# Forgetting attention: the correction matmul of the scores over all 128 rows instead of 64, in widths of at least 256 keys, with the first branch's outputs kept in DRAM

## The chip, the cores and the metric

The program runs on one core of one Trainium2 chip. The metric is the time of one execution on the device in microseconds (us); for a kernel it is the median of its runs. The engines are named as in the profile: PE (TensorE matmuls) with PEld (its weight loads), DVE (VectorE), ACT (ScalarE), POOL (GpSimd), SP (SyncE, which here only issues transfers).

## What is computed

One post-norm decoder layer over 1024 tokens of width 1024. Three causal token mixers run on one input projection: A, a gated delta rule (4 heads); B, forgetting attention (8 heads of 64); C, gated linear attention (4 heads). Their outputs are projected, merged by gates and projected once more; memory cross-attention and a routed mixture of experts follow. The part that the change touches is B:

```python
logits = (jnp.einsum('bqhd,bkhd->bhqk', q_blk, kf) * (dh ** -0.5)
          + c_blk[..., :, None] - cum_k[:, :, None, :])
logits = jnp.where(key_pos[None, :] <= query_pos[:, None], logits, -jnp.inf)
p = jax.nn.softmax(logits, axis=-1)
return jnp.einsum('bhqk,bkhd->bqhd', p.astype(v.dtype), v)
```

It is swept in blocks of 128 queries; block number qb sees (qb + 1) * 128 keys.

## The kernel before

**Precision by splitting.** float32 products are made from two parts in the type fp32r: hi is the rounded value, lo the rest. A product is hi*hi + hi*lo + lo*hi, three matmuls into one PSUM tile. `Stream.run` (L127 to L156) makes the input projection this way: for each block of 128 weight columns and each half of the tokens, 24 matmuls of 512 columns (L142, L143, L144). It is cut into steps of six matmuls; the mixers call `k.stream.fill(n)` to put n steps between their own instructions, so that PE has work while another engine prepares the next operand.

**Forgetting attention.** Heads go in pairs, p = 0 to 3. A head is only 64 wide, so hi and lo of its queries share one tile of 128 rows: `u.Q[a]` has hi in the head's own 64 rows and lo in the other 64 (`evq`, L735). `u.K[a]` holds the keys' hi part twice, in both halves (`evk`, L742). One matmul over 128 rows (L777) thus gives (q_hi + q_lo) * k_hi. The term q_hi * k_lo comes from a second matmul into the same PSUM tile (L778), over the head's own 64 rows alone; the keys' lo part `u.kl` is one tile for both heads, each in its own half.

`fox_mix` (L766) goes through the query blocks from 7 down to 0 and through both heads in each: `scores` (L777, L778 in groups of up to 512 keys; then on DVE the bias and the row's minimum, L781, on ACT the exponential, L789, on DVE the scaling, L791), `values` (L805, 64 columns wide, for both heads of a block) and `transposed` (L798), with three stream steps at the end of each round. While pair p is worked on, the stream projects q, k and v of pair p + 1, and gates of the merge. The projection's PSUM tiles and those of `values` come from one pool of two (`pmm`).

**Merge.** While pair 3 is worked on, the stream is `Merge` in place of the projection: it splits the outputs of the branches in the order c (GLA), a (delta rule), b (attention) into hi and lo and multiplies them by their projection weights. The branches' outputs are `oT`. Those of c wait in DRAM (`k.spill = "c"`) and are loaded again (L1025); those of a wait in SBUF, in four tiles taken before the delta rule begins (L2101).

**Room.** All large tiles come from one pool of 45 tiles of 4 KB a partition (`slot`). The order of the instructions on each engine is made by a scheduler, which places what the program records; each engine then goes through its list in order, and a transfer that waits on SP holds those behind it.

Of the kernel before, what the change touches and what calls it, by code (L numbers as in the profile page):

```python
# [8 lines left out]
F32 = mybir.dt.float32  # L9
# [10 lines left out]
D = 1024  # L20
T = 1024
# [23 lines left out]
def slot(k, name, shape=(128, T), dt=F32):  # L45
    """A 4 KB tile of the one pool that all large tiles share."""
    return k.b4.tile(list(shape), dt, tag="b4", name=name)


def split(k, hi, src, lo):  # L50
    """hi + lo = src exactly, each of them an fp32r value."""
    k.nc.scalar.activation(hi, src, AF.Copy)  # L52
    k.nc.vector.tensor_tensor(lo, src, hi.bitcast(F32), op=OP.subtract)  # L53
# [15 lines left out]
def load_w(k, src, cols, nb=ND):  # L69
    """128 columns of a [128 * nb, n] matrix, split: (hi, lo) as [128 rows, nb row blocks, 128]."""  # L70
    return split_raw(k, load_raw(k, src, cols, nb), nb)


def proj_T(k, w, evac, m=128):
    """evac(half, psum[m, 512]) = (x @ w)^T for each half of the tokens."""
# [12 lines left out]
class Stream:  # L88
    """Products of blocks of 128 columns of a weight with a transposed operand, one block a job, in steps between
    which other work can be put. parts: of that operand, lists by row blocks of (hi, lo), by default of x."""  # L90
# [12 lines left out]
    def hold(self, unit):  # L103
        """No job after those of this unit is begun."""
        self.limit = self.ends[unit]

    def load(self, i):
        """Weights of the jobs up to the one after job i, and two more where they are in the large pool."""
        while len(self.w) < len(self.jobs) and (
                len(self.w) < i + 2 or (len(self.w) < i + 4 and self.jobs[len(self.w)][6] is load_big)):  # L110
            src, cols, *_, load = self.jobs[len(self.w)]
            self.w.append(load(self.k, src, cols))

    def run(self):
# [5 lines left out]
        def finish():  # L120
            """What follows the last job; with a lag, when the next one is under way."""
# [46 lines left out]
def rsqrt_steps(k, out, ss, n, eps, scale=1.0, name=None):  # L168
    """Instructions for out = (scale * ss + eps) ** -0.5 on [128, n], by Newton steps from the exponent's guess."""
# [17 lines left out]
def setup(k, ins):  # L187
# [3 lines left out]
    # rows of parameters, turned into columns by one transpose  # L191
# [17 lines left out]
    k.tri = misc[:, 3]                                           # [j, i]: 1 where j <= i  # L209
# [4 lines left out]
def param_columns(k):  # L214
# [5 lines left out]
    # 0.5 from silu's tanh form, sqrt(128) from the mean of the squares  # L220
# [4 lines left out]
def alloc_T(k, half, name="th"):  # L225
    """(hi, lo) of half the tokens of a transposed [1024, tokens] operand: pairs of row blocks of [128, 2, 512]."""
# [3 lines left out]
def transpose_row(k, row, xT, t):  # L230
    """Token block t (natural, [128, 1024]) into its half of the transposed operand, split."""
# [12 lines left out]
def load_x(k, x):  # L244
    """x, transposed and split; the stream's first products come between."""
# [23 lines left out]
def small_block(k, ins):  # L269
    """The narrow columns of w_in: beta and decays of GDN, forget gates of fox, low rank of GLA."""  # L270
# [15 lines left out]
    # --- GDN: token columns of b and a  # L286
# [9 lines left out]
    gb = k.const.tile([128, 2, NT, 4], F32, name="gb")          # G (cumulative), beta  # L296
    # beta = 1 / (1 + exp(-b))
# [13 lines left out]
    # log1p(e) = 2 atanh(e / (2 + e)), e <= 1  # L311
# [21 lines left out]
    # row forms through DRAM: row (what, chunk, head)  # L333
# [8 lines left out]
    # --- fox: minus the cumulative log forget gate, in rows 64..71; GLA: log gates (times 16) of the two pairs of heads  # L342
# [27 lines left out]
    # -log f = ln(1 + exp(-|z|)) - min(z, 0)  # L370
# [16 lines left out]
def gdn_setup(k):  # L387
# [6 lines left out]
    k.negm = masks[:, 7]                                         # [j, i]: 0 where j <= i, NEG elsewhere  # L394
    nc.gpsimd.memset(k.negm, 0.0)
    nc.gpsimd.affine_select(k.negm, k.negm, [[1, 128]], OP.is_ge, NEG, base=0, channel_multiplier=-1)
    # what the inverse by blocks of 32 rows takes: L^T's diagonal blocks, four times over, and columns of T^T's
# [3 lines left out]
    # and its operands that are zero outside of the diagonal blocks of 32  # L401
# [9 lines left out]
# words of a chunk's [128, 128] in DRAM, so that its four diagonal blocks and the next chunk's are equally far apart  # L411
# [7 lines left out]
def blocks32(flat, g):  # L419
    """Rows g, g + 4, .. of the diagonal blocks [(chunk, block), 8, 32]."""  # L420
# [44 lines left out]
def gdn_mix(k, u, h, oT):  # L465
# [8 lines left out]
    # row forms of G and beta of the head  # L474
# [35 lines left out]
    def norms(y, scale, name, keep=()):  # L510
        """1 / norm of scale ** 0.5 * y by tokens; keeps y in natural form."""
# [12 lines left out]
    # k: to natural form, normalised, and back  # L524
# [9 lines left out]
    def with_k(xT, out, by, places=((slice(0, 128), slice(0, 4)),)):  # L534
        """out = (k times x)^T, weighted."""
# [9 lines left out]
    # L^T with its column blocks of 32 in the order 0, 2, 3, 1  # L545
    LT = c3(G.LT)
    with_k(kT, LT, BB, ((slice(0, 64), slice(0, 4, 3)), (slice(64, 128), slice(1, 3))))
    # T = (I + L)^-1; Tt is its transpose. The diagonal blocks of 32 rows by substitution, a quarter of the columns of
    # T on each quarter of the partitions
# [12 lines left out]
    # beta * v in natural form  # L562
# [4 lines left out]
    # q is left as it is, and the output divided by its norm  # L567
    rq = norms(yq, 128.0, "g_rq")
    # k with the decay to the chunk's end; q with the decay from its start
# [17 lines left out]
    # and the others by doubling the inverted diagonal blocks: blocks 3 and 1 of 32 rows by 2 and 0, of T in Te, of T^T  # L587
    # in Tp
    b = [slice(32 * i, 32 * i + 32) for i in range(4)]
    Te, Tp, Xp = G.Te, G.Tp, G.Xp  # L590
    Tu, X = c3(G.X[:, 0:HALF]), c3(G.X[:, HALF:])                # T's upper half of 64, and L T of it
# [32 lines left out]
    # the scan over the chunks  # L624
# [31 lines left out]
    finish_out(k, on, u.sz, 74, oT, c3(G.X))  # L656


def finish_out(k, on, sz, wc, oT, sq, spill=None):
    """RMS norm over the 128 features of on [tok, chunk, 128], times silu, transposed into oT."""  # L660
# [20 lines left out]
def fox_tiles(k, i):  # L681
    """Operands of one pair of heads; there are two sets."""
# [3 lines left out]
    F.kl.append(slot(k, "f_kl", dt=F32R))  # L686
# [9 lines left out]
def fox_setup(k):  # L696
# [4 lines left out]
    # minus the cumulative log forget gate of a head, in all rows  # L701
# [7 lines left out]
def fox_bias(k, p, a, b):  # L709
    """Loads it, for head a of pair p, from key block b up to where it has been loaded."""  # L710
# [4 lines left out]
def fox_mask(k, qb, a):  # L715
    """Masks it for query block qb; only blocks before that are read without afterwards."""
# [4 lines left out]
def fox_proj(k, ins, p, u):  # L721
    """Pair p of heads. Head 0 has its hi parts in rows 0..63 of Q and lo in 64..127, head 1 reversed."""
# [19 lines left out]
    def evk(half, ps):  # L742
        s = slice(half * HALF, (half + 1) * HALF)
        for a, own, other in ((0, up, dn), (1, dn, up)):
            nc.scalar.copy(u.K[a][own, s], ps[own])
            nc.vector.tensor_tensor(u.kl[own, s], ps[own], view(u.K[a], F32)[own, s], op=OP.subtract)
# [19 lines left out]
def fox_mix(k, u, p, oT):  # L766
# [3 lines left out]
    def scores(qb, a):  # L770
        own = (up, dn)[a]
# [3 lines left out]
        for g in range((n + 511) // 512):  # L775
            ks = slice(g * 512, min(n, g * 512 + 512))
            nc.tensor.matmul(S[:, ks], u.Q[a][:, qs], u.K[a][:, ks], start=True, stop=False)  # L777
            nc.tensor.matmul(S[:, ks], u.Q[a][own, qs], u.kl[own, ks], start=False, stop=True)  # L778
# [41 lines left out]
def gla_set(k):  # L820
    """Operands of a pair of heads."""
# [65 lines left out]
def gla_mix(k, u, p, oT):  # L887
# [15 lines left out]
    ee = k.sm.tile([128, NT, 2], F32, tag="l_ee", bufs=2)         # decay over each chunk of 64  # L903
# [7 lines left out]
    nc.vector.tensor_tensor(u.k, L.E, u.k, op=OP.mult)        # k decayed to its chunk's end  # L911
    kd = c3(u.k)
    k.stream.fill(8)
    # intra-block scores, transposed: [j, i]
# [11 lines left out]
    # q decayed from its block's start, k decayed to its block's end  # L926
# [39 lines left out]
def early_gates(k, ins, n):  # L966
    """The next n gates, kept in DRAM until the merge."""
# [13 lines left out]
class Merge:  # L981
    """Twice the gated sum of the projected branches, as a transposed operand (hi, lo by halves), and w_out; in steps
    as those of Stream."""
# [90 lines left out]
def row_tile(k, name, tag=None):  # L1074
    """A 4 KB tile in the room of the weight stream."""
# [11 lines left out]
def layer_norm(k, row, gb, eps):  # L1087
    """In place on [128 tokens, 1024]."""
# [15 lines left out]
def out_weights(k, wsrc, n):  # L1104
    """Half n of the columns of a [1024, 1024] matrix: pairs of row blocks [128, 2, 512]."""
# [15 lines left out]
def out_ln(k, m, w, resid, rscale, eps, gb, post, last=None):  # L1121
    """post(block, LN(rscale * resid + m @ w)) by blocks of 128 tokens, one block behind the products; last() comes
    before the last of them."""
# [26 lines left out]
def load_wb(k, src, cols):  # L1150
    """load_w with the raw tile from the large pool."""
# [9 lines left out]
def load_big(k, src, cols):  # L1161
    """load_w in the large pool."""
# [24 lines left out]
def xattn_proj(k, ins, S):  # L1187
    """Jobs for k transposed [f, m] and v natural [m, f] of the memory, and for q / 16 transposed, all of them split."""
# [47 lines left out]
def xattn_scores(k, u, h, half):  # L1236
    """Softmax of a head for half of the tokens: [128 tokens, 4 blocks, 256]."""
# [22 lines left out]
def xattn_values(k, u, h, Pa):  # L1260
    """The head's output, transposed and split, for one half of the tokens: (hi, lo) of [128, 2 row blocks, 512]."""
# [21 lines left out]
def route_setup(k, ins):  # L1283
# [4 lines left out]
    k.tabs = big[:, 288:352].rearrange("p (f e) -> p f e", f=2)  # of slot p of expert e: token, weight / alpha  # L1288
    k.key = big[:, 384:400].rearrange("p (t k) -> p t k", k=2)   # of each assignment: rank * 32 + expert
# [13 lines left out]
    # tokens less the one out of range, which the sum over no assignment gives a slot  # L1303
# [4 lines left out]
    k.before = r.tile([128, 128], BF, name="r_before")           # [j, i]: 1 where j < i  # L1308
# [11 lines left out]
    # of x2 = (z - mean) / dev * g + b: logits = (z @ gW - mean * sum(gW)) / dev + bW + bias  # L1320
# [22 lines left out]
def route_rows(k, r, z, g):  # L1343
    """Columns g * 512 .. of z, the rows of a block of tokens before its LN, transposed into r."""
# [17 lines left out]
def route_choose(k, r, t, dev, nb):  # L1362
    """The group and the two experts of block t's tokens, in two steps; dev, nb = 1 / deviation, - mean / deviation."""
# [9 lines left out]
    # the group: largest of 4, lowest index first; its softmax value  # L1373
# [11 lines left out]
    # the two best experts of the group  # L1385
# [826 lines left out]
```

## Time and profile before

| | before |
|---|---|
| time, median of 3 runs | 2068.1 us (2060.88 to 2074.62) |
| span of the profiled execution (first to last instruction) | 2068.5 us |
| PE busy | 1904.4 us, 92% of the span |
| DVE, ACT, POOL busy | 1212.7, 842.4, 245.1 us (59%, 41%, 12%) |
| mean granted clock of TensorE | 0.968 |
| PE from 690 to 1112 us (attention) | 422.0 of 422 us |
| PE from 1800 us to the end (experts, last norm) | 184.3 of 268 us |

The profile gives no time of the profiled execution beside its span; the span is 0.4 us above the median of the runs. In rows of instructions a duration of a matmul is not its cost: matmuls are pipelined, the next one starts before the last has ended, and the cost is the distance from one start to the next. "Idle before" names what an engine waited for. "issue" is a wait for nothing that the profile shows.

### The profile page before, as it was taken

How to read it: one execution, taken by the hardware profiler on the slowest of the kernel's cores; microseconds unless marked ns; L12 is line 12 of the kernel's file. 1: busy time of each engine (PE TensorE's matmuls, PEld its weight loads, DVE VectorE, ACT ScalarE, POOL GpSimd, SP SyncE). 2: the span in 40 equal slices, each digit the busy share in tenths (PEclk: the TensorE clock that was granted, in tenths of full speed). 3: DMA queues.
4: the chain of work that ended last, by engine and by line, in shares of the span. 5: the costliest groups of instructions: out<-in, count | busy, mean ns of one | idle time of the engine just before them, and what ended most of it. 6: DMA issues, size and time to landing. Idle time of an engine off the chain costs nothing. (4 is left out here: it accounts for less than half of the span.)

```text
span 2068.5 us, 26461 instructions
## 1 busy us (share of the span) xinstructions
PE 1904.4 (92%) x9820; PEld 1515.9 (73%) x9820; DVE 1212.7 (59%) x2604; ACT 842.4 (41%) x1446; POOL 245.1 (12%) x270
## 2 busy tenths in 40 slices
PE   7999999999999999999999999999999688988880
PEld 6777787787877777777777787988777466766660
DVE  3344377676765432323456767434677467977777
ACT  3532333333333343434433313423412267866663
POOL 2000000000000010100005000000011222432213
PEclk9999999999999999999999999999999799999995
DMA  4113132222223122122515413700444887999984
GB/s 126 32 32 82 41 95 74 74 75 74 75 67 85 49 57 77 37 77 57 190 45 194 148 69 113 196 11 14 163 167 165 267 248 219 296 271 284 301 252 164
DMA packets 233268, 261.75 MB, mean 127 GB/s; under 512 B 24362, under 2 KB 197608, under 8 KB 233136
## 3 DMA queue, kind: packets, MB, share of 16 engines
q1 hardware_dynamic: 153248, 146.30, 22.9%
q10 hardware_dynamic: 66624, 85.02, 12.5%
q0 software_dynamic: 13264, 28.71, 6.1%
q8 instruction: 78, 1.28, 0.3%
q14 instruction: 54, 0.44, 0.1%
HBM read 226.86 MB, written 49.87 MB: 134 GB/s over the span
## 5 line engine op out<-in xcount | busy, mean ns | idle before, releaser
L142 PE MATMUL ps<-thh,hi 128*128 128x512 f32 x1152 | 466.7, 405 | 1.3 <-DVE f_Q L739 1.2
L143 PE MATMUL ps<-thl,hi 128*128 128x512 f32 x1152 | 455.3, 395 | 0.0
L144 PE MATMUL ps<-thh,lo 128*128 128x512 f32 x1152 | 455.1, 395 | 0.0
L1877 DVE TENSOR_TENSOR sl<-m_raw,sh 128x1024 fp32r<-128x1024 f32 x180 | 214.8, 1222 | 66.0 <-ACT sh L1874 56.1
L142 PEld LDWEIGHTS ps<-thh,hi 128*128 128x128 f32 x1152 | 217.4, 189 | 48.3 <-issue 6.9
L144 PEld LDWEIGHTS ps<-thh,lo 128*128 128x128 f32 x1152 | 216.9, 188 | 45.8 <-issue 1.1
L143 PEld LDWEIGHTS ps<-thl,hi 128*128 128x128 f32 x1152 | 217.4, 189 | 38.6 <-DVE thl L53 0.3
L1874 ACT ACTIVATE sh<-m_raw 128x1024 fp32r<-128x1024 f32 x180 | 185.9, 1061 | 52.8 <-DMA m_raw<-in_moe_w_up 19.4
L53 DVE TENSOR_TENSOR lo<-raw,hi 128x1024 fp32r<-128x1024 f32 x64 | 78.4, 1224 | 121.4 <-ACT hi L52 120.8
L52 ACT ACTIVATE hi<-raw 128x1024 fp32r<-128x1024 f32 x64 | 67.9, 1061 | 136.5 <-PE ps L143 121.3
L1637 PE MATMUL ps<-sl,m_xhi 128*128 128x512 f32 x240 | 99.4, 414 | 18.7 <-DVE sl L1877 18.6
L781 DVE CUSTOM_DVE_ANT_0 f_P<-S,f_c 128x1024 f32<-128x1024 f32 (+7 forms) x64 | 48.4, 757 | 101.1 <-PE S L778 99.3
L1636 PE MATMUL ps<-sh,m_xhi 128*128 128x512 f32 x240 | 102.4, 427 | 5.0 <-ACT sh L1874 4.3
L1638 PE MATMUL ps<-sh,m_xlo 128*128 128x512 f32 x240 | 97.3, 406 | 1.7 <-DVE m_xlo L1896 1.7
L1696 POOL DMA_INDIRECT acc<-m_y,r_big x32 | 64.4, 2011 | 215.4 <-ACT m_y L1690 53.6
L789 ACT ACTIVATE f_P<-f_P,nm 128x1024 f32<-128x1024 f32 (+7 forms) x64 | 50.0, 781 | 79.1 <-DVE nm L781 78.9
L1051 PE MATMUL ps<-ohi,hi 128*128 128x512 f32 x192 | 76.4, 398 | 1.5 <-DVE mt L1059 1.5
L1053 PE MATMUL ps<-ohi,lo 128*128 128x512 f32 x192 | 75.1, 391 | 0.0
L1052 PE MATMUL ps<-olo,hi 128*128 128x512 f32 x192 | 75.1, 391 | 0.0
L1637 PEld LDWEIGHTS ps<-sl,m_xhi 128*128 128x128 f32 x240 | 46.7, 195 | 35.0 <-DVE sl L1877 26.3
L718 POOL TENSOR_SCALAR_AFFINE_SELECT f_c<-f_c 128x128 f32<-128x128 f32 x64 | 21.7, 339 | 404.2 <-DVE nm L781 373.0
L799 ACT COPY f_PT<-ps 128x512 f32<-128x512 f32 (+3 forms) x96 | 43.5, 481 | 56.5 <-PE ps L798 52.1
(494 smaller groups left out, 3757.6 us busy)
## 6 DMA issues: line engine op xcount, KB each, us to landing
raw<-in_w_in SPq DMA_DIRECT2D x64, 512.0 KB
m_raw<-in_moe_w_gate ACTq DMA_DIRECT2D x108, 256.0 KB
m_raw<-in_moe_w_up ACTq DMA_DIRECT2D x108, 256.0 KB
m_raw<-in_moe_w_down ACTq DMA_DIRECT2D x54, 512.0 KB
gate<-gt SPq DMA_DIRECT2D x24, 512.0 KB
mt<-gate SPq DMA_DIRECT2D x24, 512.0 KB
wraw<-in_xa_wkv SPq DMA_DIRECT2D x16, 512.0 KB
m_raw<-in_moe_w_gate SPq DMA_DIRECT2D x20, 256.0 KB
```

What stands on the lines that cost most here:

```text
L53: k.nc.vector.tensor_tensor(lo, src, hi.bitcast(F32), op=OP.subtract)
L142: k.nc.tensor.matmul(ps[:, :n], hi[:, d], xh, start=(d == 0), stop=False)
L143: k.nc.tensor.matmul(ps[:, :n], hi[:, d], xl, start=False, stop=False)
L144: k.nc.tensor.matmul(ps[:, :n], lo[:, d], xh, start=False, stop=(d == ND - 1))
L1051: nc.tensor.matmul(ps, whi[:, f], hi[:, s], start=(f == 0), stop=False)
L1052: nc.tensor.matmul(ps, whi[:, f], lo[:, s], start=False, stop=False)
L1053: nc.tensor.matmul(ps, wlo[:, f], hi[:, s], start=False, stop=(f == 3))
L1636: nc.tensor.matmul(ps, x[0], w[0], start=start, stop=False)
L1637: nc.tensor.matmul(ps, x[0], w[1], start=False, stop=False)
L1638: nc.tensor.matmul(ps, x[1], w[0], start=False, stop=stop)
L1874: nc.scalar.activation(w[e, i][0], raw[e][i], AF.Copy)
L1877: nc.vector.tensor_tensor(w[e, i][1], raw[e][i], w[e, i][0].bitcast(F32), op=OP.subtract)
```

## The change

- `evk` writes the keys' lo part into both halves, and there is one such tile for each head: `F.kl` is now a list of two, in each of two sets. This is one DVE instruction more for each head and half of the tokens.
- The second score matmul uses all rows, so that it gives (q_hi + q_lo) * k_lo.
- A group of fewer than 256 keys is made 256 wide. That concerns the 128 keys left over in query block 4, and block 0. The columns in excess are not read.
- The outputs of branch a go to DRAM as those of c do: `gdn_mix` takes a tile when it is at the end of a head and stores it, and the merge loads it again.

```diff
 def fox_tiles(k, i):
-    F.kl.append(slot(k, "f_kl", dt=F32R))
+    F.kl.append([slot(k, "f_kl", dt=F32R) for a in range(2)])
...
         for a, own, other in ((0, up, dn), (1, dn, up)):
             nc.scalar.copy(u.K[a][own, s], ps[own])
-            nc.vector.tensor_tensor(u.kl[own, s], ps[own], view(u.K[a], F32)[own, s], op=OP.subtract)
+            for rows in (own, other):
+                nc.vector.tensor_tensor(u.kl[a][rows, s], ps[own], view(u.K[a], F32)[own, s], op=OP.subtract)
             nc.scalar.copy(u.K[a][other, s], ps[own])
...
     def scores(qb, a):
-        own = (up, dn)[a]
...
-            ks = slice(g * 512, min(n, g * 512 + 512))
+            ks = slice(g * 512, min(max(n, g * 512 + 256), g * 512 + 512))
             nc.tensor.matmul(S[:, ks], u.Q[a][:, qs], u.K[a][:, ks], start=True, stop=False)
-            nc.tensor.matmul(S[:, ks], u.Q[a][own, qs], u.kl[own, ks], start=False, stop=True)
+            nc.tensor.matmul(S[:, ks], u.Q[a][:, qs], u.kl[a][:, ks], start=False, stop=True)
...
-    finish_out(k, on, u.sz, 74, oT, c3(G.X))
+    finish_out(k, on, u.sz, 74, slot(k, "oa"), c3(G.X), oT)
...
-    k.early, k.spill = {}, "c"
+    k.early, k.spill = {}, "ca"
...
-    oT = {"b": [], "c": [k.dr.tile([128, T], F32, name=f"o_c{h}") for h in range(4)]}
+    oT = {"b": [], **{b: [k.dr.tile([128, T], F32, name=f"o_{b}{h}") for h in range(4)] for b in "ac"}}
...
-        oT["a"] = [slot(k, "oa") for h in range(4)]
```

The lists of PE and DVE show where the scheduler answered. PE, pair 0, behind the scores of block 3's first head, while the stream is past the keys of pair 1 (`f_PT,f_v` is `values`, which needs the PSUM tile that `evk` still reads); first before:

```order
L798 MATMUL ps<-ident,f_P 128x128 x4
L142 MATMUL ps<-thh,hi 128x512
L143 MATMUL ps<-thl,hi 128x512
L144 MATMUL ps<-thh,lo 128x512
L142 MATMUL ps<-thh,hi 128x512
L143 MATMUL ps<-thl,hi 128x512
L144 MATMUL ps<-thh,lo 128x512
L142 MATMUL ps<-thh,hi 128x512
L143 MATMUL ps<-thl,hi 128x512
L805 MATMUL ps<-f_PT,f_v 64x128 x10
```

and the end of the same stretch in the changed kernel:

```order
L144 MATMUL ps<-thh,lo 128x512
L142 MATMUL ps<-thh,hi 128x512
L143 MATMUL ps<-thl,hi 128x512
L144 MATMUL ps<-thh,lo 128x512
L142 MATMUL ps<-thh,hi 128x512
L807 MATMUL ps<-f_PT,f_v 64x128 x10
L143 MATMUL ps<-thl,hi 128x512
```

`values` now stands behind thirteen stream matmuls where it stood behind eight. DVE at the same place, before:

```order
L746 TENSOR_TENSOR f_kl<-ps,f_K 64x512
L781 ISA f_P,nm<-S,f_c 128x512
L781 ISA nm 128x1
L746 TENSOR_TENSOR f_kl<-ps,f_K 64x512
L790 RECIPROCAL sm<-sm 128x1
```

and changed:

```order
L748 TENSOR_TENSOR f_kl<-ps,f_K 64x512 x2
L783 ISA f_P,nm<-S,f_c 128x512
L783 ISA nm 128x1
L748 TENSOR_TENSOR f_kl<-ps,f_K 64x512 x2
L792 RECIPROCAL sm<-sm 128x1
```

Each subtraction became two with nothing between them. SP at the end of the delta rule's first head, in the changed kernel:

```order
L58 DMA raw<-in_w_in 128x8x128
L678 DMA o_a_75<-oa 128x1024
L980 DMA gate_4_110<-gt 128x1024
L58 DMA raw<-in_w_in 128x8x128
L554 DMA g_blocks_2093<-g_LT 32x8x32 x4
```

The store of the branch is the new row (the others stood in this order before); the stream's next weights (`raw`) and the transfers of the next head's inverse (`g_blocks`) are queued behind it.

## Rows read from the trace of the kernel before

**Rows 1.** Busy time by engine in the attention stage; the first row names the columns.

```profile
core 0: us, PE busy (x) PEld busy (x) DVE busy (x) ACT busy (x) POOL busy (x), PEclk, DMA share, GB/s
690.00:1112.00 422.00, 422.00 (x2312) 322.40 (x2312) 173.46 (x361) 178.85 (x366) 39.78 (x87) 1.00 0.28 84
```

**Rows 2.** Lines L777 and L778: count, duration ns min/median/max, first and last start, forms.

```profile
L777 PE MATMUL S<-f_K,f_Q x96: 220/388/505, 693.4 to 1111.4; 128*128 128x512 f32 x48, 128*128 128x384 f32 x16, 128*128 128x256 f32 x16, 128*128 128x128 f32 x16
...
L778 PE MATMUL S<-f_kl,f_Q x96: 323/466/502, 693.7 to 1111.5; 64*128 64x512 f32 x48, 64*128 64x384 f32 x16, 64*128 64x256 f32 x16, 64*128 64x128 f32 x16
```

**Rows 3.** Timeline of PE, block 7: start us, us, line, tile (rows*columns), operand.

```profile
803.20 0.39 PE L144 MATMUL ps<-thh,lo 128*128 128x512 f32 x1
803.43 0.39 PE L777 MATMUL S<-f_K,f_Q 128*128 128x512 f32 x1
803.75 0.50 PE L778 MATMUL S<-f_kl,f_Q 64*128 64x512 f32 x1
804.17 0.49 PE L777 MATMUL S<-f_K,f_Q 128*128 128x512 f32 x1
804.60 0.50 PE L778 MATMUL S<-f_kl,f_Q 64*128 64x512 f32 x1
805.03 0.50 PE L142 MATMUL ps<-thh,hi 128*128 128x512 f32 x1
805.36 0.39 PE L143 MATMUL ps<-thl,hi 128*128 128x512 f32 x1
```

**Rows 4.** Timeline of PE, block 6, its second group of 384 keys.

```profile
816.61 0.44 PE L777 MATMUL S<-f_K,f_Q 128*128 128x384 f32 x1
816.98 0.43 PE L778 MATMUL S<-f_kl,f_Q 64*128 64x384 f32 x1
817.35 1.10 PE L798 MATMUL ps<-ident,f_P 128*128 128x128 f32 x8
```

**Rows 5.** Timeline of PE, block 0: 128 keys.

```profile
893.83 0.22 PE L777 MATMUL S<-f_K,f_Q 128*128 128x128 f32 x1
893.98 0.33 PE L778 MATMUL S<-f_kl,f_Q 64*128 64x128 f32 x1
894.23 0.44 PE L798 MATMUL ps<-ident,f_P 128*128 128x128 f32 x2
```

**Rows 6.** Timeline of PE, cross-attention scores: 256 columns over 128 rows.

```profile
1410.73 0.28 PE L1247 MATMUL S<-xa_kT,xa_qh 128*128 128x256 f32 x1
1410.85 0.28 PE L1248 MATMUL S<-xa_kT,xa_qh 128*128 128x256 f32 x1
```

**Rows 7.** Timeline, pair 0: keys of pair 1 leave PSUM, and the next `values`.

```profile
753.75 0.68 DVE L746 TENSOR_TENSOR f_kl<-ps,f_K 64x512 fp32r<-64x512 f32 x1 [1.39 <-ACT f_K L745]
...
756.72 0.58 ACT L747 CAST f_K<-ps 64x512 fp32r<-64x512 f32 x1
...
757.16 0.40 PE L143 MATMUL ps<-thl,hi 128*128 128x512 f32 x1
...
757.48 1.31 PE L805 MATMUL ps<-f_PT,f_v 128*64 128x128 f32 x20
```

**Rows 8.** Timeline of DVE and PE: the scaled scores of block 7, and their transposes.

```profile
808.37 0.75 DVE L791 TENSOR_SCALAR f_P<-f_P,sm 128x1024 f32<-128x1024 f32 x1
...
810.82 1.09 PE L798 MATMUL ps<-ident,f_P 128*128 128x128 f32 x8
```

**Rows 9.** Timeline of DVE: the output of the delta rule's first head.

```profile
394.90 1.41 DVE L676 SCALAR_TENSOR_TENSOR oa<-ps,pcol,g_sz 128x512 f32<-128x512 f32 x2
```

**Rows 10.** Timeline of SP at that time.

```profile
392.30 0.37 SPq L58 DMA_DIRECT2D raw<-in_w_in  x1
404.47 0.34 SPq L978 DMA_DIRECT2D gate<-gt  x1
405.20 0.37 SPq L58 DMA_DIRECT2D raw<-in_w_in  x1
408.03 1.32 SPq L554 DMA_DIRECT2D g_blocks<-g_LT  x3
```

**Rows 11.** Timeline: branch c loaded again for the merge, issue (SP) and first split (ACT).

```profile
1003.60 0.32 SPq L1025 DMA_DIRECT2D oraw<-o_c  x1
...
1008.24 1.06 ACT L52 ACTIVATE ohi<-oraw 128x1024 fp32r<-128x1024 f32 x1 [2.82 <-DMA oraw<-o_c]
```

## The prediction

> **What bounds the kernel now.** I read the busy time by stretch first, since the change lies in one stage. In the attention stage PE is busy for all of its 422 us, while DVE is busy for 173 and ACT for 179, some 42% each [rows 1]. So whatever PE saves there is time saved, until something that hides behind PE comes late. The granted clock is 1.00 throughout, the upper of the two levels, 2.4 GHz. Next I read the two score lines: 96 matmuls each, of which 48 are 512 keys wide, and 16 each 384, 256 and 128 [rows 2]. The line with 64 rows lasts longer than the one with 128 (median 466 against 388 ns), although it has half the rows. Durations overlap, so the third view is the order of time on PE, from start to start.
>
> There the matter shows plainly [rows 3]. A matmul of 512 columns behind another with the same tile takes 0.23 us (803.20 to 803.43). The 128-row score matmul that has a 64-row one behind it takes 0.32 (803.43 to 803.75); between two of these it takes 0.43 (804.17 to 804.60), and so does the 64-row one (804.60 to 805.03). The first stream matmul after it takes 0.33 (805.03 to 805.36). Each change between 128*128 and 64*128 costs PE about 0.1 us on either side of it. The extra does not shrink with the width: at 384 keys each of the two takes 0.37 [rows 4], at 128 keys 0.15 and 0.25 [rows 5]. This is not a cost of accumulating in one PSUM tile: L142 to L144 do that too, at 0.23.
>
> The Trainium skill states the same cause ("TensorEngine Tiling (Array Packing)", section Tiling Modes): changing the tiling mode drains the engine. The trace agrees, with 0.43 against 0.23 us.
>
> **What PE saves.** One head of one pair makes 12 groups over its eight query blocks, and there are 8 such passes (8 * 12 = 96). I price a group from the start of its L777 to the start of what follows its L778.
>
> - 512 keys: 0.74 for the first group of a block (803.43 to 804.17), 0.86 for the second (804.17 to 805.03). A pass has five first ones and one second: 5 * 0.74 + 0.86 = 4.56.
> - 384 keys: 0.74 as second group [rows 4]; as first group 0.12 less, the difference just seen: 0.62. Together 1.36.
> - 128 keys: 0.40 as first [rows 5], 0.52 as second. Together 0.92.
> - 256 keys: midway between these, 0.51 and 0.63. Together 1.14.
>
> That is 7.98 us a pass and 63.8 us in all. Afterwards every matmul here has the tile of its neighbours. At 512 columns it costs 0.23, at 256 columns 0.12 [rows 6], at 384 midway, 0.175. The former 128-key groups are 256 wide too. A pass: 6 * 0.46 + 2 * 0.35 + 4 * 0.24 = 4.42 us, and 35.4 in all. **PE saves 28.4 us.** Of this the widening takes something back: rows 5 against rows 6 give no sign that 128 columns are dear (0.15, of which 0.1 is the change of tile), so 32 matmuls grow by about 0.06, which is 2 us and already in the sum.
>
> Behind the group two small things run against each other. Stream matmuls and transposes that followed a 64-row matmul lose up to 0.1 us each, a gain. Where `values` follows, the tile still changes, to 128*64, and that entry costs 0.09 (757.16 to 757.48 is 0.32 and not 0.23 [rows 7]), which I counted as saved. I take a gain of 1 us, bounds -2 to +3.
>
> **What it adds.** Sixteen more subtractions on DVE at 0.68 us [rows 7] are 11 us of DVE. In a stage where DVE is 41% busy they hide behind PE, except in one place. `evk` goes back and forth between ACT and DVE (own rows on ACT, subtraction on DVE, other rows on ACT, for one head and then the other), and its PSUM tile comes free at the end. Now that is 2 * 0.68 = 1.4 us later. Before, the last ACT copy ended at 757.30 and `values` began at 757.48: PE came just in time [rows 7]. Six times in the stage (three pairs, two halves) this can turn into a wait of up to 1.4 us: 0 to 8 us. In the changed list `values` stands five stream matmuls later at the place shown, worth 5 * 0.23 = 1.15 us, so most is covered; but PE arrives there about 0.4 us sooner, a group being cheaper. I take 0.3 us each, 2 us in all. Pair 0 leaves PSUM during the delta rule, beside a chain on DVE; there the two subtractions inside that chain are as many as before.
>
> The store of branch a takes 0.3 us of SP four times, and it waits for DVE, ahead of weights and of `g_blocks`. The output is complete at 396.3 [rows 9]; SP issues nothing between 392.7 and 404.5, and the next weights at 405.2 [rows 10]. So the store has gone 8 us before anything behind it is due: nothing. It costs room for one tile a head instead of four throughout; with two more for the keys, the pool is less full. I credit nothing, since PE does not wait in the stage.
>
> The reload for the merge is four transfers and four waits on ACT and DVE for them. For branch c the first one came 4.6 us after its issue, and ACT stood 2.8 us [rows 11] while PE went on [rows 1]. Two merge jobs of 24 matmuls (11 us) lie between the loading and the first use. I take 1 us, bounds 0 to 6 (one landing and one split more than can be hidden).
>
> **Sum.** 2068.5 - 28.4 - 1 + 2 + 1 = 2042 us. The span is what I count from; the median of the runs is 0.4 us below it, and nothing measurable lies around it. With all bounds at their ends the forecast itself covers 2035 to 2056.
>
> **The rivals.**
>
> *The waits come out.* With up to 0.8 us less in each round, the softmax chain, which PE hid, may become late. The scaled scores of block 7 are ready at 809.12, and their transposes start at 810.82 [rows 8]: a margin of 1.7 us, which shrinks to 0.9. Rounds in which DVE also has a split of 1.2 us or the longer evacuation are the tight ones. Against it: the smaller blocks save less and their chain is shorter. If PE gave back 0.25 us in 48 of the 64 rounds, that is 12 us: 2054. Chance 0.16.
>
> *The height is not the cause.* If the 0.43 belonged to the second operand's matmul for another reason, such as its weights being a part of the tile that L777 has just loaded, then nothing is saved on the 64-row side and the widening costs 2 us, with the 2 us of evacuation: 2072. For it speaks that half the rows should not be dearer; against it, that the 128-row matmuls beside them pay the same, and that `values`, another tile shape, pays 0.09 on entry [rows 7]. Chance 0.04. The Trainium skill has a rule on this side ("TensorEngine Tiling (Array Packing)", section Performance Considerations): a contraction of 64 should be tiled by rows, two at a time. No two 64-row matmuls stand together here, so no run shows that gain.
>
> *The queue of SP holds the weights.* The stores stand in order ahead of weights and `g_blocks`. Where a head's output came more than 8 us later relative to the stream than at 396.3, the store would hold the weights, and PE would run dry in the delta rule. It ends slower from about 8 us of stall at four heads beyond that margin, 32 us and more: 2042 + 36 = 2078. The rows speak against it [rows 9, 10]. Chance 0.03.
>
> **Chances and range.** The forecast's case, 2034 to 2049, has 0.77. About 1%, 21 us, is what a measurement can tell from no change here, as the three runs lie 14 us apart. Below 2047 are most of the first case and a part of the first rival: faster by over 1% 0.80; within 1% 0.16; slower by over 1% 0.04. The range 2033 to 2055 takes in the bounds and most of the first rival and leaves out the other two.
>
> **What would show it.** From start to start L780 (the old L778) should take 0.23 us at 512 keys, and the matmul before it too. PE's attention stage should shrink from 422 us to about 395 and still be full. If L807 (`values`) or the matmuls behind the merge's reload show waits of a microsecond, the additions were priced too low. If L780 still takes 0.43, the cause was another. The stages before and after should keep their lengths within a few microseconds; a delta rule that grows would speak for SP.

## The result and the profile after

| | before | after |
|---|---|---|
| time, median of 11 runs each | 2062.7 us (2060.1 to 2074.6) | 2050.4 us (2045.6 to 2058.4) |
| profiled execution: time, span | not recorded, 2068.5 us | 2051.0, 2049.3 us |
| PE busy | 1904.4 us | 1876.2 us |

The ratio is 0.9933, with an interval of 0.9915 to 0.9951: 14 us faster, 10 to 18 (the medians lie 12.3 us apart). 2042 us were forecast, with 2033 to 2055 as the range. What was forecast of PE came, and then a third of it was lost again in one place.

First the score lines. They moved down by two lines (L777 to L779, L778 to L780); the columns are those of [rows 2].

```profile
L779 PE MATMUL S<-f_K,f_Q x96: 277/388/499, 692.3 to 1091.7; 128*128 128x512 f32 x48, 128*128 128x256 f32 x32, 128*128 128x384 f32 x16
...
L780 PE MATMUL S<-f_kl,f_Q x96: 277/389/420, 692.5 to 1091.8; 128*128 128x512 f32 x48, 128*128 128x256 f32 x32, 128*128 128x384 f32 x16
```

The median duration of the second line falls from 466 ns to 389, which is that of the first line. From the first score matmul to the last it is now 399.4 us (692.3 to 1091.7); before, 418.0 [rows 2]. In the order of time on PE, block 7, which answers to [rows 3], with the transposes behind it:

```profile
801.25 0.39 PE L779 MATMUL S<-f_K,f_Q 128*128 128x512 f32 x1
801.48 0.39 PE L780 MATMUL S<-f_kl,f_Q 128*128 128x512 f32 x1
801.71 0.39 PE L779 MATMUL S<-f_K,f_Q 128*128 128x512 f32 x1
801.93 0.39 PE L780 MATMUL S<-f_kl,f_Q 128*128 128x512 f32 x1
802.16 1.03 PE L800 MATMUL ps<-ident,f_P 128*128 128x128 f32 x8
```

Every start is 0.22 to 0.23 us behind the one ahead of it, where [rows 3] had 0.32 and 0.43. The four matmuls take 0.91 us (801.25 to 802.16) in place of 1.60. The distance from one start to the next, the pitch, is 0.17 us at 384 keys, where it was 0.37 [rows 4]; at 256 keys it is 0.11 to 0.12, as in [rows 6].

But PE is not full in the stage any more, and the prediction had it full, at about 395 us. The busy time by stretch, first of the stage [rows 1], then of its last part in steps of 10 us, with the columns of [rows 1]:

```profile
690.00:1093.00 403.00, 395.77 (x2312) 325.38 (x2310) 180.00 (x370) 179.41 (x366) 41.33 (x87) 0.99 0.31 93
...
1040.00:1050.00 10.00, 10.00 (x64) 8.33 (x59) 4.93 (x12) 4.87 (x11) 0.98 (x2) 1.00 0.20 74
1050.00:1060.00 10.00, 5.19 (x28) 3.98 (x26) 7.50 (x17) 5.58 (x10) 1.39 (x3) 0.95 0.06 25
1060.00:1070.00 10.00, 8.71 (x43) 7.22 (x44) 2.52 (x4) 1.24 (x3) 0.00 (x0) 0.70 0.33 92
```

The first column is the stretch, then come its length and PE's busy time in it. Of the 7.2 us that PE stands in the stage (403.00 - 395.77), 6.1 lie between 1050 and 1070 us, where the merge's products and the last pair of heads share PE. From 1060 to 1070 us the mean granted clock is 0.70; in the kernel before it is 1.00 throughout [rows 1]. The waits of PE from 690 to 1190 us say for whom it stood (total us, times, longest; two of 0.3 and 0.2 us in all are left out):

```profile
PE ps L807 <- DVE msum L1059: 4.2, 1, 4.2
PE ps L800 <- DVE f_P L793: 1.7, 2, 1.5
PE S L779 <- DVE nm L783: 1.7, 1, 1.7
PE ps L1053 <- DVE mt L1061: 1.5, 1, 1.5
PE ps L807 <- DVE mt L1061: 0.8, 1, 0.8
```

In the kernel before, the fourth was the only one. The largest: `values` (L807) needs a tile of PSUM, the memory that matmuls write, from the pool of two, and both hold products of the merge that DVE's sum `msum` (L1059) has not yet read. The timeline of PE there:

```profile
1054.61 0.28 PE L780 MATMUL S<-f_kl,f_Q 128*128 128x256 f32 x1
1056.61 0.39 PE L779 MATMUL S<-f_K,f_Q 128*128 128x256 f32 x1 [1.72 <-DVE nm L783]
1056.83 0.28 PE L780 MATMUL S<-f_kl,f_Q 128*128 128x256 f32 x1
1061.29 2.40 PE L807 MATMUL ps<-f_PT,f_v 128*64 128x128 f32 x20 [4.18 <-DVE msum L1059]
1063.62 0.80 PE L1053 MATMUL ps<-ohi,hi 128*128 128x512 f32 x1
1064.21 0.63 PE L1054 MATMUL ps<-olo,hi 128*128 128x512 f32 x1
1064.64 0.63 PE L1055 MATMUL ps<-ohi,lo 128*128 128x512 f32 x1
...
1065.49 0.59 PE L1054 MATMUL ps<-olo,hi 128*128 128x512 f32 x1
1065.92 0.40 PE L1055 MATMUL ps<-ohi,lo 128*128 128x512 f32 x1
```

And DVE in that time:

```profile
1045.75 0.69 DVE L1059 SCALAR_TENSOR_TENSOR msum<-mt,ps 128x512 f32<-128x512 f32 x1 [2.04 <-PE ps L1055]
...
1049.44 1.23 DVE L53 TENSOR_TENSOR olo<-oraw,ohi 128x1024 fp32r<-128x1024 f32 x1 [0.26 <-ACT ohi L52]
1051.44 0.69 DVE L783 CUSTOM_DVE_ANT_0 f_P<-S,f_c 128x512 f32<-128x512 f32 x1 [0.77 <-PE S L780]
...
1053.62 0.56 DVE L783 CUSTOM_DVE_ANT_0 f_P<-S,f_c 128x384 f32<-128x384 f32 x1
...
1054.71 1.31 DVE L53 TENSOR_TENSOR olo<-oraw,ohi 128x1024 fp32r<-128x1024 f32 x1
...
1058.28 2.36 DVE L53 TENSOR_TENSOR olo<-oraw,ohi 128x1024 fp32r<-128x1024 f32 x2 [0.33 <-ACT ohi L52]
1060.55 1.28 DVE L1059 SCALAR_TENSOR_TENSOR msum<-mt,ps 128x512 f32<-128x512 f32 x2
```

PE had filled the two tiles by 1049.3 and 1052.95 us. The sums that empty them stand in DVE's list behind all four splits of the reloaded tiles (`olo<-oraw`, 4.9 us of work) and behind softmax steps of three later score blocks (the lines shown are some of them), and they start at 1060.55. The last issue on SP for these tiles was at 1047.7 us and the slowest of the four took 8.0 us to land: by 1055.7 at the latest they all lay in SBUF, the memory that ACT and DVE read here, and the last two splits began at 1058.28. It is DVE's list, not the landing, that ends last.

The price: PE stood 4.18 + 1.72 = 5.9 us. Then it ran at the lower clock: the 20 matmuls of L807 take 2.33 us to the next start, where they took 1.24 at 752.75 us in the same trace, and the five merge matmuls from 1063.62 take 2.30, where at the upper clock the first takes about 0.33 behind `values` and the others 0.23 (1.25). Together 5.9 + 1.1 + 1.1 = 8.1 us.

### The profile page after: what moved, and what is told of

Read it like the earlier page. It is cut to its first block, busy times and chain, and to the rows that moved or that the text cites. A ratio compares the mean times of both kernels' runs of the same rounds, so it can differ in the third digit from the quotient of the medians.

```text
span 2049.3 us, 26495 instructions
## 1 busy us (share of the span) xinstructions
PE 1876.2 (92%) x9820; PEld 1517.6 (74%) x9820; DVE 1222.0 (60%) x2620; ACT 841.8 (41%) x1446; POOL 242.1 (12%) x270
## 5 line engine op out<-in xcount | busy, mean ns | idle before, releaser
L1639 PE MATMUL ps<-sl,m_xhi 128*128 128x512 f32 x240 | 99.2, 413 | 16.2 <-DVE sl L1879 16.2
L1698 POOL DMA_INDIRECT acc<-m_y,r_big x32 | 56.9, 1777 | 212.9 <-ACT m_y L1692 55.7
L1054 PE MATMUL ps<-olo,hi 128*128 128x512 f32 x192 | 75.2, 392 | 0.0
```

Of the source, the lines that this page charges most:

```text
L1054: nc.tensor.matmul(ps, whi[:, f], lo[:, s], start=False, stop=False)
L1639: nc.tensor.matmul(ps, x[0], w[1], start=False, stop=False)
```

## The experiments

To compare stretches I use one length in every profile: from the start of the first score matmul to the start of the merge's last hi-lo matmul (L1054 after). It holds the whole of the change's work but the stores. Each ratio is to runs of the kernel before that were made beside it.

| kernel | first to last, us | length | ratio to before (interval) |
|---|---|---|---|
| before | 693.4 to 1184.0 | 490.6 | 1 |
| after | 692.3 to 1166.7 | 474.4 | 0.9933 (0.9915 to 0.9951) |
| b_spill | 692.8 to 1190.8 | 498.0 | 1.0062 (1.0041 to 1.0083) |
| a_k64 | 694.0 to 1197.6 | 503.6 | 1.0105 (1.0080 to 1.0129) |
| a_noload | 692.0 to 1157.7 | 465.7 | 0.9882 (0.9855 to 0.9909) |
| a_sp4567 | 692.1 to 1157.7 | 465.6 | 0.9883 (0.9860 to 0.9906) |
| a_sp67 | 693.5 to 1167.0 | 473.5 | 0.9926 (0.9905 to 0.9948) |
| b_grouped | 693.2 to 1171.9 | 478.7 | 0.9951 (0.9932 to 0.9969) |
| a_nowide | 699.5 to 1173.8 | 474.3 | 0.9923 (0.9899 to 0.9947) |
| a_best | 693.8 to 1159.6 | 465.8 | 0.9883 (0.9856 to 0.9910) |

Theory 1: the height gave all that was forecast, and the reload of branch a lost part of it through the place of the sums on DVE. Theory 2: the softmax chain, now less covered, took it.

**b_spill: the reload alone, on the kernel before.**

```diff
-    finish_out(k, on, u.sz, 74, oT, c3(G.X))
+    finish_out(k, on, u.sz, 74, slot(k, "oa"), c3(G.X), oT)
...
-    k.early, k.spill = {}, "c"
+    k.early, k.spill = {}, "ca"
...
```

What is left out is the DRAM tiles of `oT`, as in the change.

> The kernel before, with one part of the change alone: branch a's four tiles are stored to DRAM and read back in the merge; the score matmuls stay as they were. Theory 1 (the merge gives back about 10 us, because with the reload the sums that free the two PSUM tiles of the products stand on VectorE behind the splits of the reloaded tiles): 8 to 12 us slower than the kernel before, a ratio of 1.004 to 1.006, with a wait of some 4 us of PE at the values of the attention near the end of it and a low granted clock behind it. Theory 2 (what was not gained was lost to the softmax chain, which the shorter scores lay bare, and the reload costs nothing): the time of the kernel before, 0.999 to 1.001.

Measured 1.0062, a little above the ratio that theory 1 named, and 7.4 us more in the stretch, a little below its 8 to 12. The waits of PE in the same stretch as above, with L777 and L805 for L779 and L807:

```profile
PE ps L805 <- DVE msum L1057: 4.0, 1, 4.0
...
PE S L777 <- DVE nm L781: 1.3, 1, 1.3
```

The two waits of the changed kernel are there (4.0 and 1.3 against 4.2 and 1.7), with the old 64-row scores. From 1080 to 1090 us its granted clock is 0.73. Theory 2 is out as the main cause: no score has become shorter here.

**a_noload: the changed kernel, branch a's splits read a resident tile.**

```diff
-            if b in k.spill:
+            if b == "a":
+                x = k.resident
+            elif b in k.spill:
                 x = slot(k, "oraw")
                 nc.sync.dma_start(x, oT[b][f])
+                k.resident = x
```

> The changed kernel without the reload of branch a: its four splits read a tile that is resident (the last tile of branch c that was reloaded), so branch a's products are computed on the wrong data; the stores stay. Everything else is as in the changed kernel. Theory 1: the sums stand between the splits on VectorE again, PE does not wait for them, and the time is 8 to 12 us below the changed kernel, 0.987 to 0.990 of the kernel before. Theory 2 (softmax chain): the time of the changed kernel, 0.993 within 0.001.

Measured 0.9882; the stretch is 8.7 us shorter than in the changed kernel. As many splits run on DVE, and neither the wait for `msum` nor that for `nm` is left. On DVE the steps stand as before the change: one split, a sum, three splits, and then the sums singly among the softmax steps. The splits' own work costs nothing that shows. But this kernel takes away the transfers and the order at once; the next one parts them.

**a_sp4567: reload and split one tile a job.**

```diff
...
-        if n < 2 and j == ND - 2:
-            operands(n + 1)
+        if n == 0 and j in {4: (0,), 5: (1,), 6: (2,), 7: (3,)}:
+            operands(1, {4: (0,), 5: (1,), 6: (2,), 7: (3,)}[j])
+        if n == 1 and j == ND - 2:
+            operands(2)
```

`operands` takes the list of tiles as a second argument.

> The changed kernel with the reload and split of branch a's four tiles spread over the merge's jobs 4 to 7, one tile each, instead of all four at job 6. Theory 1: one split stands between two sums on VectorE, PE does not wait 4 us for them, and 6 to 11 us of the loss come back: 0.987 to 0.991 of the kernel before. The rival that the reload itself (its transfers, its place on the queue) costs the 10 us, whatever the order of the splits: the time of the changed kernel, 0.993.

Measured 0.9883, 8.8 us less in the stretch than after, with all four transfers in it. The timeline of DVE (the lines are two further down than after: L1061 is the sum):

```profile
1048.94 1.23 DVE L53 TENSOR_TENSOR olo<-oraw,ohi 128x1024 fp32r<-128x1024 f32 x1 [0.26 <-ACT ohi L52]
1050.09 0.68 DVE L1061 SCALAR_TENSOR_TENSOR msum<-mt,ps 128x512 f32<-128x512 f32 x1
...
1054.39 0.69 DVE L1061 SCALAR_TENSOR_TENSOR msum<-mt,ps 128x512 f32<-128x512 f32 x1 [0.89 <-PE ps L1057]
...
1058.06 1.22 DVE L53 TENSOR_TENSOR olo<-oraw,ohi 128x1024 fp32r<-128x1024 f32 x1
1059.19 0.68 DVE L1061 SCALAR_TENSOR_TENSOR msum<-mt,ps 128x512 f32<-128x512 f32 x1
```

A sum follows each split, and from 1045.55 on no two sums are more than 4.8 us apart, where it was 14.8 (1045.75 to 1060.55). PE is full from 1040 to 1080 us at a clock of 1.00. This kernel's time is 2040.1 us, and the reload as such costs nothing that shows.

**a_sp67: two tiles at each of two jobs.** The same edit with `{6: (0, 1), 7: (2, 3)}`.

> A half dose: the changed kernel with the reload and split of branch a's four tiles at jobs 6 and 7, two each. On VectorE two sums then stand behind two splits, and two more behind the next two, where in the changed kernel two stand behind four. Theory 1 (what the sums stand behind decides): part of the loss comes back, 0.9885 to 0.9925 of the kernel before, with waits of PE for the sums that are each shorter than 4.2 us. The rival that the loss comes of having any split of a reloaded tile among the softmax steps: the time of the changed kernel, 0.993.

Measured 0.9926: a miss, just above the range named, and only 0.9 us of the loss came back. The waits:

```profile
PE ps L1055 <- DVE msum L1061: 2.9, 1, 2.9
PE ps L807 <- DVE msum L1061: 1.8, 1, 1.8
...
PE ps L1055 <- DVE sm L792: 0.9, 1, 0.9
```

Each wait for a sum is shorter, as theory 1 has it, but there are two, and with the 0.9 they are as long as before (5.6 against 5.9 us). So the loss does not go with the number of splits between two sums, and theory 1 has no rule for its size. Between them there also stand softmax steps of later blocks, which wait for PE and ACT in turn, and two pairs of sums were held up in place of one. What part each has in the 5.6 us was not tried.

**a_k64: the second matmul over 64 rows again, and no more.**

```diff
-            nc.tensor.matmul(S[:, ks], u.Q[a][:, qs], u.kl[a][:, ks], start=False, stop=True)
+            own = (up, dn)[a]
+            nc.tensor.matmul(S[:, ks], u.Q[a][own, qs], u.kl[a][own, ks], start=False, stop=True)
```

> The changed kernel with the second score matmul over its own 64 rows again, and nothing else undone. The theory that the change of the tile's height made PE drain (0.2 us in each of 80 groups of 512 or 384 columns, less in the narrower ones, 28 us in all): 24 to 30 us slower than the changed kernel, 1.004 to 1.008 of the kernel before, and the pitch around the second matmul of a 512-column group 0.43 us instead of 0.23. The rival that the height costs nothing by itself and the gain came with the other order of the work: the time of the changed kernel, 0.993.

Measured 1.0105, and 29.2 us more in the stretch than after. The ratio is above the forecast one, the length within it: the profiled execution was the fastest of six, 7 us below their median, and where that spread lies was not looked for. (Of the groups, 64 and not 80 have 512 or 384 columns [rows 2].) Block 7 on PE:

```profile
805.11 0.39 PE L779 MATMUL S<-f_K,f_Q 128*128 128x512 f32 x1
805.43 0.50 PE L781 MATMUL S<-f_kl,f_Q 64*128 64x512 f32 x1
805.85 0.50 PE L779 MATMUL S<-f_K,f_Q 128*128 128x512 f32 x1
806.28 0.50 PE L781 MATMUL S<-f_kl,f_Q 64*128 64x512 f32 x1
806.71 0.50 PE L142 MATMUL ps<-thh,hi 128*128 128x512 f32 x1
```

These are the pitches of [rows 3] again: 0.32, 0.42, 0.43, 0.43. The height alone does it, with nothing else undone, so the rival that the height is not the cause is out.

**b_grouped: the kernel before, with the matmuls of a block in another order.**

```diff
             nc.tensor.matmul(S[:, ks], u.Q[a][:, qs], u.K[a][:, ks], start=True, stop=False)
+        for g in range((n + 511) // 512):
+            ks = slice(g * 512, min(n, g * 512 + 512))
             nc.tensor.matmul(S[:, ks], u.Q[a][own, qs], u.kl[own, ks], start=False, stop=True)
```

> The kernel before, with the matmuls of a block in another order: first the 128-row matmuls of all its groups, then the 64-row ones, so that a block of more than 512 keys (32 of the 64) has two changes of height instead of four. Nothing else differs, no reload. The theory that each change of height costs about 0.1 us on each side of it (0.2 us of pitch a change): 9 to 13 us faster than the kernel before, 0.9935 to 0.996. The rival that a matmul of 64 rows is slow in itself, wherever it stands: the time of the kernel before, 0.999 to 1.001.

Measured 0.9951, and 11.9 us less in the stretch. Block 7 on PE:

```profile
805.64 0.61 PE L777 MATMUL S<-f_K,f_Q 128*128 128x512 f32 x2
806.19 0.76 PE L780 MATMUL S<-f_kl,f_Q 64*128 64x512 f32 x2
806.88 1.09 PE L800 MATMUL ps<-ident,f_P 128*128 128x128 f32 x8
```

Four matmuls, two of them still of 64 rows, take 1.24 us (805.64 to 806.88) where they took 1.60 [rows 3]. 32 such blocks at 0.36 make 11.5. So a 64-row matmul is not slow in itself: the change from one height to the other is. (None stands between two others of 64 rows in any run; with only one neighbour of another height it has about 0.34, with two 0.43.) The Trainium skill ("TensorEngine Tiling (Array Packing)", section Tiling Modes) states that such a change drains the engine. This run and a_k64 agree as far as time can show it, at 0.2 us a change.

**a_nowide and a_best: without the minimum of 256 keys.** In the changed kernel, and in a_sp4567.

```diff
-            ks = slice(g * 512, min(max(n, g * 512 + 256), g * 512 + 512))
+            ks = slice(g * 512, min(n, g * 512 + 512))
```

> The changed kernel without the minimum of 256 keys: the 32 matmuls of the last query block of each head have 128 columns again. If a matmul of 128 columns costs what its columns cost (pitch 0.06 us against 0.11 to 0.12): 1 to 2 us faster than the changed kernel, which this comparison can hardly tell from it, 0.992 to 0.993. If 128 columns of this type are dear (a multiple of the pitch): up to 6 us slower, 0.994 to 0.996. The stage of the attention in the profile tells the two apart.

> A version that may beat both kernels: the changed kernel with the splits of branch a spread over jobs 4 to 7 and without the minimum of 256 keys. If the two edits add up: 2038 to 2040 us, 0.986 to 0.989 of the kernel before, with an attention stage some 1 to 2 us below the 390.5 us of the spread alone. If narrow matmuls are dear: 2040 to 2045.

Measured 0.9923 and 0.9883. Both are within the ratios named, but a_best's 2041.4 us are above the 2038 to 2040, and the 1 to 2 us of the stage are not there: 474.3 against 474.4 us, and 465.8 against 465.6. The timeline of a_nowide shows half of why:

```profile
887.24 0.22 PE L779 MATMUL S<-f_K,f_Q 128*128 128x128 f32 x1
887.29 0.28 PE L780 MATMUL S<-f_kl,f_Q 128*128 128x128 f32 x1
887.41 0.41 PE L800 MATMUL ps<-ident,f_P 128*128 128x128 f32 x2
```

The first matmul of 128 columns takes 0.05 us, but the second 0.12, what 256 columns take. So 128 columns save just under 0.06 once a group, 16 times: 0.9 us. The other half: PE's waits at L807 for the evacuated keys rise from 0.2 to 1.1 us. a_best beats both kernels, but a_sp4567 does it as well with one edit less.

## Why the forecast was right, and where it failed

**What bounds the kernel, and the 28.4 us: right.** The pitches forecast (0.23, 0.175, 0.12) are those measured. In a_sp4567, where the clock is 1.00 in the whole stretch, PE's busy time there is 28.2 us less than before (489.1 to 460.9); the forecast had 28.4, and 1 for what stands behind the groups. a_k64 puts the height alone at 29.2 us, with its narrow groups 256 wide as well; by the prediction's prices that is 30.2. The 28.2 us between the two figures of PE busy in the first table are another sum and agree by chance: 25.5 of them lie in the stretch and 4.3 ahead of it, where the seven runs with the scores at L779 range from 664.0 to 671.8 us.

**The widening's 2 us, and the gain of 1 us at entry and exit: nearly nothing.** The widening costs 0.9 (a_nowide). `values` behind a score still pays the change to its 64 columns: 0.33 us in place of 0.23 at 512, 0.27 in place of 0.17 at 384.

**The evacuation's 2 us: the right place, and smaller.** PE's weight loads wait for the keys six times, as forecast, for 2.9 us in all, where they waited 1.3 before. But a weight load overlaps the matmul ahead of it, so the cost is the distance to the start of `values`:

```profile
752.26 0.39 PE L142 MATMUL ps<-thh,hi 128*128 128x512 f32 x1
752.75 1.31 PE L807 MATMUL ps<-f_PT,f_v 128*64 128x128 f32 x20
753.99 0.50 PE L143 MATMUL ps<-thl,hi 128*128 128x512 f32 x1
```

Here it is 0.49 us, where [rows 7] had 0.32. Before, all such starts behind a stream matmul have 0.32 or 0.33, whether the load waited or not; after, five of eight have more, 0.37 to 0.52. That is 0.7 us in all. In a_k64, with the same subtractions, all have 0.32 again: they show only where PE comes sooner, as the prediction argued.

**The stores: right.** On SP's timeline the first one, and what comes next there:

```profile
395.79 0.34 SPq L678 DMA_DIRECT2D o_a<-oa  x1
403.89 0.34 SPq L980 DMA_DIRECT2D gate<-gt  x1
```

The gate comes 0.6 us sooner than in [rows 10], and the store is long gone. The first score matmul, which stands behind nearly all of the delta rule, starts at 692.3 us where it started at 693.4: the delta rule did not grow, and the rival of SP's queue is out.

**The reload's "1 us, bounds 0 to 6": wrong, and the step that failed.** It cost 8.8 us in the changed kernel (against a_sp4567; 8.7 against a_noload) and 7.4 in the kernel before (b_spill), beyond its own bound. The prediction asked what waits for the landing: "four transfers and four waits on ACT and DVE for them", with two merge jobs, 11 us, as cover. Neither waited for a landing of these tiles: the one wait of ACT for `oraw`, 2.3 us, is for branch c. But with the reload the scheduler put the splits, together with later softmax steps, ahead of the sums that empty PSUM, and the cover was only as deep as the two tiles of `pmm`: PE filled both and stood. The prediction looked for who waits for the splits, and not for who stands behind them on DVE. Both lists of DVE could be read before the run; the price could not. The prediction's own sign for it did come: a wait of a microsecond and more at L807 (4.2). And the wait did not come alone: the lower clock behind it added 2.2 us to 5.9. Why the scheduler moved them was not tried; the lists differ between a_noload and after, by the transfer alone.

**"The waits come out": the wrong place, and small.** Its sentence, 0.25 us given back in 48 rounds, is not what happened. At the end of the stage there are two waits, L800 for the scaled scores (1.5 us) and L807 for `mt` (0.8). They remain in a_noload and a_sp4567, so they are no part of the reload's loss, and a_k64 has them too (1.2 and 0.8), so they do not come of shorter scores; a_nowide has them, so they do not come of the widening. They are in none of before, b_spill and b_grouped. What brings them, the keys' second lo tile or the order that comes with it, stays open.

**The sum.** In the stretch the change saves 490.6 - 474.4 = 16.2 us. a_sp4567, without the loss behind the reload, saves 25.0; with the waits at the end (2.3) and at the evacuation (0.7) put back, PE's own saving is 28.0. So 28.0 - 8.8 - 2.3 - 0.7 = 16.2, where the forecast had 28.4 + 1 - 1 - 2 = 26.4. Of the 10.2 between them 7.8 is the reload, 2.3 the end and 1.4 PE's saving, less 1.3 of the evacuation. The bounds given add up to 2037 to 2056 us, and not to 2035.

**The time: inside the range, in part by luck.** 2050.4 us lie in 2033 to 2055, but above the forecast's own case (2034 to 2049, chance 0.77); and 0.7% faster is what was called no change (within 1%, chance 0.16), not the "faster by over 1%" that had 0.80. The upper part of the range was there for the reload's bound and for the first rival; the bound was passed, and the rival's mechanism is not what happened. The start was high as well: the forecast counts from a span of 2068.5 us, and over 11 runs the median time of before is 2062.7. Against that 2042 would be 21 us and not 26. Counted from that median the same sum gives 2036, 14 us off instead of 8: the high start hid a part of the miss. Nor is the time below the span, as the prediction took it: in every run with both on record it is 1.7 or 1.8 us above it.

## What to carry to other kernels

A change of tile height between neighbouring matmuls cost 0.2 us here at every width from 128 to 512 columns; put matmuls of one height together first (b_grouped: 12 us of the stretch for an order that needs no room), and even the height out where the room is there. When an operand that was resident is loaded again, look in the list of the engine that prepares it for what now stands behind it, above all for instructions that give PSUM back, and spread the work so that one of these comes between two pieces (a_sp4567: 2040.1 us).

## What the runs showed of the hardware

- Half the rows are no cheaper, and apart from the changes no dearer: in b_grouped two 128-row and two 64-row matmuls of 512 columns take 1.24 us, in the changed kernel four of 128 rows 0.91. Two changes of height at 0.2 us, the last partly in the pitch of what follows, are the difference.
- A pitch of 0.32 stands also where the tile is 128*128 on both sides: at the first stream matmul behind the transposes L800 (802.95 to 803.27 us after, 0.23 from there). So height is not the only change that costs about 0.1 us; what it is there was not tried.
- Of two matmuls of 128 columns in a row the second takes 0.12 us, and the first 0.05 (a_nowide). The weight load of what follows begins late there, 0.04 us ahead of its matmul; that it sets the 0.12 was not tried:

```profile
887.24 0.19 PEld L780 LDWEIGHTS S<-f_kl,f_Q 128*128 128x128 f32 x1
887.37 0.20 PEld L800 LDWEIGHTS ps<-ident,f_P 128*128 128x128 f32 x2
```

- In the changed kernel PE stood for 5.9 of the 6.4 us from 1054.89 to 1061.29. Then the mean granted clock was 0.70 from 1060 to 1070 us, a part of that time at the lower level of 1.2 GHz: the pitch at 512 columns is 0.43 us until 1065.92 and 0.23 from there. So the pause cost 2.2 us more after it had ended.
